# Gates, merges and the merged sum with tokens on partitions: activations stand still, weights pass 512 columns wide

## The chip, the cores and the metric

The kernel runs on one core of one Trainium2 chip. The metric is the device time of one execution in microseconds. A core has TensorE (PE, the matrix engine, which takes its instructions in order), VectorE (DVE), ScalarE (ACT), GpSimd (POOL) and SyncE (SP, which issues the DMA transfers here). They run side by side and wait for each other through semaphores.

## The reference

Two layers, each with a mixer of four branches and a mixture of experts, on 256 tokens (T) of 1024 channels (D). What matters here is the end of the mixer: each branch output is projected to 1024 channels, multiplied by a sigmoid gate computed from the layer's input h, and the four are added and projected once more.

```python
def hybrid_mixer(h, positions, w_in, ..., branch_proj, w_gate, w_out):
    ...
    merged = [jax.nn.sigmoid(h @ w_gate[i]) * (o.astype(h.dtype) @ branch_proj[i])
              for i, o in enumerate((o_gdn, o_ret, o_nsa, o_fox))]
    y = merged[0] + merged[1] + merged[2] + merged[3]
    return y @ w_out
```

## The kernel before, in words

Channels lie on partitions throughout the mixer: h is held as 8 blocks (k) of 128 channels by 256 tokens. Matmuls of single-precision accuracy are made of three passes in a faster format: every operand is split into a rounded part and a rest (`hh`/`hl` for h, `whi`/`wlo` for a weight, `yh`/`yl` for the merged sum, `gdnhi`/`gdnlo` and the like for a branch's output, `bhi`/`blo` for a branch's projection), and hi x hi, lo x hi and hi x lo are added in PSUM. ACT makes the rounded part of a weight and DVE the rest (`split_half`), 512 columns at a time; a part holds 1024 columns, and one part is ahead of its use.

A matmul names the operand that stands still (its weight load is an instruction of its own) and the one that passes; a profile row `ps_d<-hh,whi` has the passing one first. In the gates (`gates`, through `dense_T` and `dense_k`) the weight stands still, 128 columns of it, and 256 tokens pass: for each of the 4 branches (n) and each quarter of the channels (q) 8 x 2 x 3 = 48 matmuls of 256 columns. ACT turns the result into tanh (`sg`, sigmoid up to a factor and an addend). `merge` makes the branch's projection of that quarter (12 matmuls), and DVE multiplies it by the gate (`sg`) and adds it to the sum `ymix`; for branch 3 `fin` then writes `yh` and `yl` with ACT and DVE. The output projection w_out reads them, block k after block k.

PE's order is written by hand. The branches are generators (`gdn`, `nsa`, `ret`, `fox`) driven by `drive`; between their steps `fill` takes a fixed number of steps of the filler (`s.later`): first the remaining input projections, then the gates, with steps of the conditioning vector's matmuls (`ada`) in between. A gate step is two blocks k (12 matmuls). At most `NSG` = 5 gate results wait for their merge, which needs its branch's output (`oT[n]`). What is left when the last branch (`fox`) has ended runs without anything in between (`s.ended`), then w_out and the normalisation, then the experts. On the other engines a scheduler sets the order; weight splits have high priority there. PSUM has 8 banks, of which 3 carry the tag "d" (gates, merges, `ada`, w_out) and 2 the tag "t" (transposes). SP issues the weight loads in program order through four ring buffers; loads of expert weights (`exp_w`) follow as buffers of the mixer come free.

Of the kernel before, what the change touches and what calls it, by code (L numbers as in the profile page):

```python
# [22 lines left out]
L = 2  # L23
# [15 lines left out]
MP = 9  # L39
# [116 lines left out]
def pack(inputs):  # L156
# [20 lines left out]
    wg = i["w_gate"].reshape(L, 4, KT, 128, 4, 256).transpose(0, 1, 4, 3, 2, 5)  # L177
# [48 lines left out]
class K:  # L226
# [72 lines left out]
    def split_half(s, w, pool, bufs=2):  # L299
# [7 lines left out]
        return [t.rearrange("p (k n) -> p k n", k=4) for t in (hi, lo)]  # L307
# [7 lines left out]
    def dense_T(s, act, ps, tok=False):  # L315

        for half in range(2):
            hi, lo = s.parts.pop(0)
            s.split()
            for k4 in range(4):  # L320
                k = half * 4 + k4
                s.dense_k(hi[:, k4], lo[:, k4], k, act, ps, tok)
                if k % 2 and k < 7:
                    yield

# [216 lines left out]
    def gates(s, l, act, oT, fin):  # L542
# [7 lines left out]
        def prepare():  # L550

            if len(parts) < min(NBP, len(todo)) and todo[len(parts)] in sg and ready(todo[len(parts)][0]):
                n, q = todo[len(parts)]
                if q == 0:
                    bp[n] = s.load(s.I["bp"][l, n]).rearrange("p (k n) -> p k n", k=2)
                parts.append(s.merge_split(bp[n][:, :, q * 256:q * 256 + 256]))

        def merge():
            n, q = todo.pop(0)
            s.merge(parts.pop(0), n, q, sg.pop((n, q)), oT[n])  # L560
            if n == 3:
                fin(q)

        todo = [(n, q) for n in range(4) for q in range(4)]
        for n in range(4):
            for q in range(4):
                while len(sg) >= NSG:
# [5 lines left out]
                ps = s.ps("d")  # L573
                for i, _ in enumerate(s.dense_T(act, ps)):
                    if i in MMI and len(sg) >= MM and len(parts) >= (1 if s.ended else MP):
# [3 lines left out]
                g = s.ml.tile([128, 2, T], F32, name="sg", tag="sg", bufs=NSG)  # L579
                s.nc.scalar.activation(g, ps.rearrange("p (c n) -> p c n", c=2), AF.Tanh, scale=0.5)  # L580
                sg[n, q] = g
                yield
                if parts:
                    merge()
                    yield
# [30 lines left out]
    def start(s, hT, act, x, pool):  # L616
# [5 lines left out]
        def work(n):  # L622

            for _ in range(n):
                if todo:
                    i, k0 = todo.pop(0)
                    for k in (k0, k0 + 1):
                        if i == 3:
                            s.narrow_k(hT, w[3], pn, k)
                        else:  # L630
                            hi, lo = w[i][k // 4]
# [48 lines left out]
    def mixer(s, l, hT, act, x, residual, es):  # L680
        nc, I, tc = s.nc, s.I, s.tc
        pool = lambda name, side, bufs=1: tc.tile_pool(name=f"{name}{l}", bufs=bufs, side=side, reuse_waits="tile")
        with pool("wp", "left", 2) as s.wp, ExitStack() as ml:
            s.ml = ml.enter_context(pool("ml", "left"))
            rt = es.enter_context(pool("rt", "right"))
            with pool("fx", "left") as s.fx, ExitStack() as fy:
                with pool("mx", "right") as s.mx:
# [37 lines left out]
                    def fin(q):  # L725

                        k = slice(2 * q, 2 * q + 2)
                        nc.scalar.activation(yhl[0][:, k], s.y[:, k], AF.Copy, scale=0.5)
                        nc.vector.scalar_tensor_tensor(yhl[1][:, k], s.y[:, k], 0.5, yhl[0][:, k].bitcast(F32), op0=OP.mult, op1=OP.subtract)
# [62 lines left out]
    def merge_split(s, w):  # L792
        nc = s.nc
        hi = s.wp.tile([128, 2, 256], F32R, name="bhi", tag="bhi", bufs=NBP)
        lo = s.wp.tile([128, 2, 256], F32R, name="blo", tag="blo", bufs=NBP)
        with s.tc.high_priority(HP):
            nc.scalar.activation(hi, w, AF.Copy)
            nc.vector.tensor_tensor(lo, w, hi.bitcast(F32), op=OP.subtract)
        return hi, lo

    def merge(s, w, n, q, sg, oT):
# [4 lines left out]
        for c in range(2):  # L806
            o = ps[:, c * 256:c * 256 + 256]
            cs = slice(c * 128, c * 128 + 128)
            for k in range(2):
                s.mm(o, hi[:, k, cs], oT[0][:, k], k == 0 and c == 0, False)  # L810
                s.mm(o, hi[:, k, cs], oT[1][:, k], False, False)
                s.mm(o, lo[:, k, cs], oT[0][:, k], False, k == 1)
        yq = s.y[:, 2 * q:2 * q + 2]
        p3 = ps.rearrange("p (c n) -> p c n", c=2)
        if n == 0:
            nc.vector.scalar_tensor_tensor(yq, sg, 1.0, p3, op0=OP.add, op1=OP.mult)
        else:
            nc.vector.scalar_tensor_tensor(sg, sg, 1.0, p3, op0=OP.add, op1=OP.mult)
# [934 lines left out]
```

## Time and profile before

| | |
|---|---|
| Time, median of 3 runs | 1280.85 us (1280.41 to 1282.26) |
| The profiled execution: its time, its span | 1281.46 us, 1279.6 us |
| TensorE matmul busy | 1174.5 us, 92% of the span |
| TensorE weight load busy (beside matmuls) | 831.6 us, 65% |
| VectorE, ScalarE, GpSimd busy | 623.3, 429.0, 80.6 us (49%, 34%, 6%) |
| Mean granted TensorE clock | 0.971 of full speed |
| DMA | 347.94 MB, mean 272 GB/s |

The time is that of one execution outside; the span is what the profiler saw of it. Busy time counts matmuls in flight, so PE counts as busy also where its matmuls only overlap; how often they follow each other says more than how long each lasts.

### The profile page before, as it was taken

To read this page: it belongs to the slowest core of one execution; us is meant where nothing else is said; L and a number is where in the kernel's file an instruction comes from. 1 tells how busy PE (TensorE), PEld (TensorE's weight loads), DVE (VectorE), ACT (ScalarE), POOL (GpSimd) and SP (SyncE) were. 2 spreads that over 40 slices of the span, in tenths; PEclk is the share of its full clock that TensorE was granted. 3 is DMA by queue.
4 is the path that set the end of the run, shared out by engine and by line. 5 is a ranking of instruction groups with operands and counts; after the bars stand their busy time and mean duration, and the time that the engine had idled before them with its cause. 6 is when DMAs were issued, how large, how long until landed. Compare 5 with 4: busy or idle time off the path is not lost. (4 is left out here: it accounts for less than half of the span.)

```text
span 1279.6 us, 21410 instructions
## 1 busy us (share of the span) xinstructions
PE 1174.5 (92%) x8708; PEld 831.6 (65%) x8708; DVE 623.3 (49%) x1641; ACT 429.0 (34%) x889; POOL 80.6 (6%) x92
## 2 busy tenths in 40 slices
PE   6899998989997999999879999898999799999975
PEld 3788996788993444433367889688899644444332
DVE  3694437675665222222179644757467622222214
ACT  2443432464434211111154344245354431112101
POOL 1123200000001000000001411000000100000000
PEclk9999999999998999999889999998999899999998
DMA  9886646635778999998227563552567899999920
GB/s 365 318 295 228 214 169 236 255 132 198 275 288 349 379 420 419 419 420 361 82 102 254 205 222 131 184 206 104 226 239 279 311 391 415 418 420 419 419 77 33
DMA packets 49935, 347.94 MB, mean 272 GB/s; under 512 B 5664, under 2 KB 6176, under 8 KB 8480
## 3 DMA queue, kind: packets, MB, share of 16 engines
q1 hardware_dynamic: 49680, 346.17, 69.8%
q8 instruction: 72, 1.18, 0.4%
q14 instruction: 39, 0.32, 0.1%
q10 hardware_dynamic: 144, 0.27, 0.1%
HBM read 345.37 MB, written 1.05 MB: 271 GB/s over the span
## 5 line engine op out<-in xcount | busy, mean ns | idle before, releaser
L243 PE MATMUL ps_d<-hh,whi 128*128 128x256 f32 x864 | 258.7, 299 | 6.1 <-ACT whi L305 2.8
L243 PE MATMUL ps_d<-hh,wlo 128*128 128x256 f32 x864 | 248.7, 288 | 0.7 <-DVE wlo L306 0.7
L243 PE MATMUL ps_d<-hl,whi 128*128 128x256 f32 x864 | 248.3, 287 | 1.2 <-DVE hl L668 1.1
L306 DVE TENSOR_TENSOR wlo<-w,whi 128x512 fp32r<-128x512 f32 x264 | 181.1, 709 | 120.8 <-ACT whi L305 120.2
L305 ACT ACTIVATE whi<-w 128x512 fp32r<-128x512 f32 x264 | 155.6, 624 | 230.9 <-PE ps_d L243 210.8
L243 PEld LDWEIGHTS ps_d<-hh,whi 128*128 128x128 f32 x864 | 168.3, 195 | 19.7 <-issue 10.0
L243 PEld LDWEIGHTS ps_d<-hl,whi 128*128 128x128 f32 x864 | 168.8, 195 | 1.8 <-DVE hl L668 1.6
L243 PEld LDWEIGHTS ps_d<-hh,wlo 128*128 128x128 f32 x864 | 167.3, 194 | 1.2 <-DVE wlo L306 1.2
L243 PE MATMUL ps_a<-w,hidT 128*64 128x512 f32 x512 | 118.6, 598 | 0.0
L825 DVE SCALAR_TENSOR_TENSOR x<-ps_d,mod,x 128x256 f32<-128x256 f32 x144 | 60.4, 477 | 82.3 <-PE ps_d L243 82.3
L1505 DVE TENSOR_TENSOR hid<-hid,ps_a 128x512 f32<-128x512 f32 x16 | 11.0, 688 | 169.0 <-PE ps_a L243 169.0
L243 PEld LDWEIGHTS ps_a<-w,hidT 128*64 128x64 f32 x512 | 34.5, 136 | 59.4 <-issue 56.6
L243 PE MATMUL ps_b<-w,hb 128*64 128x512 f32 x256 | 66.4, 628 | 7.1 <-PEq L1658 7.1
L243 PE MATMUL ps_b<-w,XG 128*64 128x512 f32 x256 | 66.4, 621 | 0.0
L243 PE MATMUL ps_a<-w,XG 128*64 128x512 f32 x256 | 60.6, 594 | 0.0
L243 PE MATMUL ps_a<-w,hb 128*64 128x512 f32 x256 | 59.7, 592 | 0.0
L1536 ACT ACTIVATE oh<-ps_a,cw 128x512 fp32r<-128x512 f32 x30 | 20.6, 688 | 116.1 <-PE ps_a L243 86.1
L243 PEld LDWEIGHTS <-ha 128*128 128x128 bf16 x576 | 40.6, 100 | 24.2 <-issue 22.5
L1537 DVE SCALAR_TENSOR_TENSOR ol<-ps_a,cw,oh 128x512 fp32r<-128x512 f32 x30 | 22.4, 748 | 68.3 <-ACT oh L1536 68.3
L243 PE MATMUL ps_d<-P,ha 128*128 128x128 bf16 x512 | 49.9, 224 | 5.8 <-DVE P L1457 4.3
L996 POOL TENSOR_TENSOR C<-Lm,consm 128x512 f32<-128x512 f32 x28 | 39.3, 1422 | 93.3 <-PE ps_a L243 84.3
L243 PEld LDWEIGHTS ps_b<-w,hb 128*64 128x64 f32 x256 | 18.8, 143 | 38.2 <-issue 35.7
(433 smaller groups left out, 1945.2 us busy)
## 6 DMA issues: line engine op xcount, KB each, us to landing
w<-exp_w SPq DMA_DIRECT2D x192, 1024.0 KB, 12.2
w<-ada SPq DMA_DIRECT2D x48, 1024.0 KB, 5.2
w<-wg SPq DMA_DIRECT2D x32, 1024.0 KB, 4.8
w<-win SPq DMA_DIRECT2D x26, 1024.0 KB, 5.2
w<-cw SPq DMA_DIRECT2D x8, 1024.0 KB, 5.8
w<-bp SPq DMA_DIRECT2D x8, 1024.0 KB, 4.8
w<-wo SPq DMA_DIRECT2D x8, 1024.0 KB, 4.9
consm<-constm SPq DMA_DIRECT2D x2, 720.0 KB, 6.5
```

Of the source, the lines that this page charges most:

```text
L243: return s.nc.tensor.matmul(o, l, r, start=start, stop=stop, skip_group_check=True)
L305: nc.scalar.activation(hi[:, m], w[:, m], AF.Copy)
L306: nc.vector.tensor_tensor(lo[:, m], w[:, m], hi[:, m].bitcast(F32), op=OP.subtract)
L825: s.nc.vector.scalar_tensor_tensor(x[:, k], y[:, c * T:c * T + T], mod[:, 16 + k:17 + k], x[:, k], op0=OP.mult, op1=OP.add)
L996: nc.gpsimd.tensor_tensor(C[c], Lm[c], lm[:, lev][:, None].to_broadcast([128, 4, 128]), op=OP.mult)
L1505: nc.vector.tensor_tensor(t, t, hs[1], op=OP.mult)
L1536: nc.scalar.activation(oh[:, sl], po[:, sl], AF.Copy, scale=cw)
L1537: nc.vector.scalar_tensor_tensor(ol[:, sl], po[:, sl], cw, oh[:, sl].bitcast(F32), op0=OP.mult, op1=OP.subtract)
```

## The change

In gates and merges the activations now stand still (128 tokens of one block k, `hh[:, k, c]`) and the split weight passes, 512 columns wide. So a gate block is one branch (n), one half of the channels (f, 512 columns) and one half of the tokens (t); both halves t are made together by `dense_tok` into two PSUM banks, in 8 blocks k of 2 x 3 matmuls of 512 columns. A step is now one block k. w_gate is laid out for this (chunks of half of K by 512 columns). `merge` makes one half t with 6 matmuls of 512 columns; `merge_split` splits 512 columns of the projection at once, in two halves k, for both merges t. The sum `ymix` has tokens on partitions, and `fin`, which runs after each merge of branch 3, transposes its 512 channels with four PE transposes into a bank of tag "t", from which ACT and DVE write `yh` and `yl`. A new gate block of two results starts only while at most `NSG` - 2 wait. The scratch for software DMA is set to 1024 bytes.

```diff
-    wg = i["w_gate"].reshape(L, 4, KT, 128, 4, 256).transpose(0, 1, 4, 3, 2, 5)
+    wg = i["w_gate"].reshape(L, 4, 2, 4, 128, 2, 512).transpose(0, 1, 5, 2, 4, 3, 6)
...
+    def dense_tok(s, act, ps):
+        hh, hl = act
+        for k in range(KT):
+            if k % 2 == 0:
+                hi, lo = (t.rearrange("p (k n) -> p k n", k=2) for t in s.parts.pop(0))
+                s.split()
+            for t in range(2):
+                c = slice(t * 128, t * 128 + 128)
+                s.mm(ps[t], hh[:, k, c], hi[:, k % 2], k == 0, False)
+                s.mm(ps[t], hl[:, k, c], hi[:, k % 2], False, False)
+                s.mm(ps[t], hh[:, k, c], lo[:, k % 2], False, k == 7)
+            if k < 7:
+                yield
...
         def prepare():
-            if len(parts) < min(NBP, len(todo)) and todo[len(parts)] in sg and ready(todo[len(parts)][0]):
-                n, q = todo[len(parts)]
-                if q == 0:
+            if not parts and todo and todo[0] in sg and ready(todo[0][0]):
+                n, f, _ = todo[0]
+                if f == 0:
                     bp[n] = s.load(s.I["bp"][l, n]).rearrange("p (k n) -> p k n", k=2)
-                parts.append(s.merge_split(bp[n][:, :, q * 256:q * 256 + 256]))
+                parts.append(s.merge_split(bp[n][:, :, f * 512:f * 512 + 512]))
         def merge():
-            n, q = todo.pop(0)
-            s.merge(parts.pop(0), n, q, sg.pop((n, q)), oT[n])
+            n, f, t = todo.pop(0)
+            s.merge(parts[0], n, f, t, sg.pop((n, f, t)), oT[n])
+            if t:
+                parts.clear()
             if n == 3:
-                fin(q)
-        todo = [(n, q) for n in range(4) for q in range(4)]
+                fin(f, t)
+        todo = [(n, f, t) for n in range(4) for f in range(2) for t in range(2)]
         for n in range(4):
-            for q in range(4):
-                while len(sg) >= NSG:
+            for f in range(2):
+                while len(sg) > NSG - 2:
                     prepare()
                     yield
                     if parts:
                         merge()
                         yield
-                ps = s.ps("d")
-                for i, _ in enumerate(s.dense_T(act, ps)):
-                    if i in MMI and len(sg) >= MM and len(parts) >= (1 if s.ended else MP):
+                ps = [s.ps("d") for _ in range(2)]
+                for i, _ in enumerate(s.dense_tok(act, ps)):
+                    if i % 4 in MMI and len(sg) >= MM and parts and s.ended:
                         merge()
                     prepare()
                     yield
-                g = s.ml.tile([128, 2, T], F32, name="sg", tag="sg", bufs=NSG)
-                s.nc.scalar.activation(g, ps.rearrange("p (c n) -> p c n", c=2), AF.Tanh, scale=0.5)
-                sg[n, q] = g
+                for t in range(2):
+                    g = s.ml.tile([128, 512], F32, name="sg", tag="sg", bufs=NSG)
+                    s.nc.scalar.activation(g, ps[t], AF.Tanh, scale=0.5)
+                    sg[n, f, t] = g
                 yield
-                if parts:
-                    merge()
-                    yield
+                for _ in range(2):
+                    if parts:
+                        merge()
+                        yield
...
-                    def fin(q):
-                        k = slice(2 * q, 2 * q + 2)
-                        nc.scalar.activation(yhl[0][:, k], s.y[:, k], AF.Copy, scale=0.5)
-                        nc.vector.scalar_tensor_tensor(yhl[1][:, k], s.y[:, k], 0.5, yhl[0][:, k].bitcast(F32), op0=OP.mult, op1=OP.subtract)
+                    def fin(f, t):
+                        pt = s.ps("t")
+                        for i in range(4):
+                            s.tr(pt[:, i * 128:i * 128 + 128], s.y[:, t, f * 512 + i * 128:f * 512 + i * 128 + 128])
+                        p4 = pt.rearrange("p (k n) -> p k n", k=4)
+                        hi, lo = (y[:, 4 * f:4 * f + 4, t * 128:t * 128 + 128] for y in yhl)
+                        nc.scalar.activation(hi, p4, AF.Copy, scale=0.5)
+                        nc.vector.scalar_tensor_tensor(lo, p4, 0.5, hi.bitcast(F32), op0=OP.mult, op1=OP.subtract)
...
     def merge_split(s, w):
         nc = s.nc
-        hi = s.wp.tile([128, 2, 256], F32R, name="bhi", tag="bhi", bufs=NBP)
-        lo = s.wp.tile([128, 2, 256], F32R, name="blo", tag="blo", bufs=NBP)
+        hi = s.wp.tile([128, 2, 512], F32R, name="bhi", tag="bhi", bufs=NBP)
+        lo = s.wp.tile([128, 2, 512], F32R, name="blo", tag="blo", bufs=NBP)
         with s.tc.high_priority(HP):
-            nc.scalar.activation(hi, w, AF.Copy)
-            nc.vector.tensor_tensor(lo, w, hi.bitcast(F32), op=OP.subtract)
+            for k in range(2):
+                nc.scalar.activation(hi[:, k], w[:, k], AF.Copy)
+                nc.vector.tensor_tensor(lo[:, k], w[:, k], hi[:, k].bitcast(F32), op=OP.subtract)
         return hi, lo
-    def merge(s, w, n, q, sg, oT):
+    def merge(s, w, n, f, t, sg, oT):
         nc = s.nc
         hi, lo = w
         ps = s.ps("d")
-        for c in range(2):
-            o = ps[:, c * 256:c * 256 + 256]
-            cs = slice(c * 128, c * 128 + 128)
-            for k in range(2):
-                s.mm(o, hi[:, k, cs], oT[0][:, k], k == 0 and c == 0, False)
-                s.mm(o, hi[:, k, cs], oT[1][:, k], False, False)
-                s.mm(o, lo[:, k, cs], oT[0][:, k], False, k == 1)
-        yq = s.y[:, 2 * q:2 * q + 2]
-        p3 = ps.rearrange("p (c n) -> p c n", c=2)
+        c = slice(t * 128, t * 128 + 128)
+        for k in range(2):
+            s.mm(ps, oT[0][:, k, c], hi[:, k], k == 0, False)
+            s.mm(ps, oT[1][:, k, c], hi[:, k], False, False)
+            s.mm(ps, oT[0][:, k, c], lo[:, k], False, k == 1)
+        y = s.y[:, t, f * 512:f * 512 + 512]
         if n == 0:
-            nc.vector.scalar_tensor_tensor(yq, sg, 1.0, p3, op0=OP.add, op1=OP.mult)
+            nc.vector.scalar_tensor_tensor(y, sg, 1.0, ps, op0=OP.add, op1=OP.mult)
         else:
-            nc.vector.scalar_tensor_tensor(sg, sg, 1.0, p3, op0=OP.add, op1=OP.mult)
-            nc.vector.tensor_tensor(yq, yq, sg, op=OP.add)
+            nc.vector.scalar_tensor_tensor(sg, sg, 1.0, ps, op0=OP.add, op1=OP.mult)
+            nc.vector.tensor_tensor(y, y, sg, op=OP.add)
...
-                s.y = s.hp.tile([128, KT, T], F32, name="ymix", tag="h")
+                s.y = s.hp.tile([128, 2, D], F32, name="ymix", tag="h")
...
-    nc = bacc.Bacc("TRN2", target_bir_lowering=False, num_devices=1)
+    nc = bacc.Bacc("TRN2", target_bir_lowering=False, num_devices=1, dynamic_dma_scratch_size=1024)
```

Three places in the order. First PE at the end of layer 0's gates: `foxhi`/`foxlo` are the last branch's output, `rws` a small sum for the router, `yh`/`yl` with `whi`/`wlo` the first matmuls of w_out. Before:

```order
L243 MATMUL ps_d<-foxhi,blo 128x256
L243 MATMUL ps_d<-foxhi,bhi 128x256
L243 MATMUL ps_d<-foxlo,bhi 128x256
L243 MATMUL ps_d<-foxhi,blo 128x256
L243 MATMUL ps_b<-rws,cons 128x32
L243 MATMUL ps_d<-yh,whi 128x256 [waits Activation_49]
L243 MATMUL ps_d<-yl,whi 128x256 [waits DVE_49]
L243 MATMUL ps_d<-yh,wlo 128x256
```

Now:

```order
L243 MATMUL ps_d<-bhi,foxlo 128x512
L243 MATMUL ps_d<-blo,foxhi 128x512
L247 MATMUL ps_t<-cons,ymix 128x128 [waits DVE_49,PE_49]
L247 MATMUL ps_t<-cons,ymix 128x128 x3
L243 MATMUL ps_d<-bhi,foxhi 128x512 [waits Activation_49]
L243 MATMUL ps_d<-bhi,foxlo 128x512
L243 MATMUL ps_d<-blo,foxhi 128x512
L243 MATMUL ps_d<-bhi,foxhi 128x512
L243 MATMUL ps_d<-bhi,foxlo 128x512
L243 MATMUL ps_d<-blo,foxhi 128x512
L247 MATMUL ps_t<-cons,ymix 128x128 [waits DVE_49,PE_49]
L247 MATMUL ps_t<-cons,ymix 128x128 x3
```

Before, w_out's matmuls come directly behind the last merge; now four transposes of `ymix` stand behind each merge of this branch, and the first of them carries a wait for DVE.

Second DVE at the same place: line 818 before and line 839 now is the product of gate and projection, line 819 and 840 the sum, line 729 and 752 the part `yl`. Before:

```order
L818 SCALAR_TENSOR_TENSOR sg<-sg,ps_d 128x512 [waits PE_49]
L798 TENSOR_TENSOR blo<-w,bhi 128x512 [waits Activation_49]
L819 TENSOR_TENSOR ymix<-ymix,sg 128x512 [waits DVE_49]
L306 TENSOR_TENSOR wlo<-w,whi 128x512 [waits PE_49,Activation_49]
L729 SCALAR_TENSOR_TENSOR yl<-ymix,yh 128x512 [waits Activation_49] x3
L818 SCALAR_TENSOR_TENSOR sg<-sg,ps_d 128x512 [waits PE_49,Activation_49]
L306 TENSOR_TENSOR wlo<-w,whi 128x512 [waits Activation_49]
L819 TENSOR_TENSOR ymix<-ymix,sg 128x512 [waits DVE_49]
```

Now:

```order
L306 TENSOR_TENSOR wlo<-w,whi 128x512 [waits Activation_49]
L306 TENSOR_TENSOR wlo<-w,whi 128x512 [waits PE_49,Activation_49]
L752 SCALAR_TENSOR_TENSOR yl<-ps_t,yh 128x4x128 [waits Activation_49] x2
L839 SCALAR_TENSOR_TENSOR sg<-sg,ps_d 128x512 [waits PE_49]
L306 TENSOR_TENSOR wlo<-w,whi 128x512 [waits Activation_49]
L840 TENSOR_TENSOR ymix<-ymix,sg 128x512 [waits DVE_49]
L752 SCALAR_TENSOR_TENSOR yl<-ps_t,yh 128x4x128 [waits Activation_49]
L839 SCALAR_TENSOR_TENSOR sg<-sg,ps_d 128x512 [waits PE_49]
L840 TENSOR_TENSOR ymix<-ymix,sg 128x512 [waits DVE_49]
```

Before, three `yl` are written from `ymix` ahead of the last product; now two `yl` are written from transposes in PSUM ahead of the product of the merge before the last, behind which that merge's transposes wait.

Third PE in the middle of layer 0, in the compression of the sparse attention (`w,bk`) and the rotation of the retention's keys and queries (`ps_b<-c`). Before:

```order
L243 MATMUL ps_t<-w,bk_2169 32x256 x2
L243 MATMUL ps_t<-w,bk_2177 32x256 x2
L243 MATMUL ps_b<-c_106 128x256
L243 MATMUL ps_b<-c_106 128x128
L243 MATMUL ps_b<-c_106 128x256
L243 MATMUL ps_b<-c_106 128x128
L243 MATMUL ps_d<-hh,whi 128x256
L243 MATMUL ps_d<-hl,whi 128x256
L243 MATMUL ps_d<-hh,wlo 128x256
```

Now:

```order
L243 MATMUL ps_b<-c_106 128x256
L243 MATMUL ps_b<-c_106 128x128
L243 MATMUL ps_b<-c_106 128x256
L243 MATMUL ps_b<-c_106 128x128
L243 MATMUL ps_t<-w,bk_2104 32x256 x2
L243 MATMUL ps_t<-w,bk_2112 32x256 x2
L243 MATMUL ps_t<-w,bk_2104 32x256 x2
L243 MATMUL ps_t<-w,bk_2112 32x256 x2
L243 MATMUL ps_b<-c_106 128x256
```

Before, 24 gate matmuls (the last three rows are the first of them) stand between the `ps_b<-c` and the next `w,bk`; now the next `w,bk` follows at once, since four gate results wait already, and the gates that stood here come later in the program.

## Rows read from the trace of the kernel before

**Rows 1.** The page, its first part: busy us (share of the span) xinstructions.

```profile
PE 1174.5 (92%) x8708; PEld 831.6 (65%) x8708; DVE 623.3 (49%) x1641; ACT 429.0 (34%) x889; POOL 80.6 (6%) x92
```

**Rows 2.** Windows of layer 0's gate stretch: length, busy us of each engine (instructions), granted clock, DMA.

```profile
150.00:240.00 90.00, 84.73 (x736) 72.48 (x735) 48.55 (x105) 31.50 (x60) 4.06 (x7) 0.98 0.62 228
240.00:290.00 50.00, 45.85 (x356) 41.81 (x356) 38.31 (x144) 29.27 (x88) 0.00 (x0) 0.97 0.39 144
...
338.00:356.00 18.00, 17.98 (x151) 17.78 (x150) 13.03 (x22) 8.47 (x16) 0.00 (x0) 1.00 0.71 255
```

**Rows 3.** PE's waits from 150 to 356 us: total us, times, longest.

```profile
PE ps_a L243 <- DVE stn L1293: 4.0, 4, 2.8
PE ps_b L243 <- DVE c L1124: 2.9, 2, 2.0
```

**Rows 4.** Experts of layer 0: a window, and SP's timeline (start, us, operation, count).

```profile
480.00:512.00 32.00, 31.93 (x199) 14.16 (x200) 9.13 (x25) 5.53 (x12) 0.00 (x0) 1.00 1.01 420
...
379.90 210.65 SPq L262 DMA_DIRECT2D w<-exp_w  x83
```

**Rows 5.** Window of 10 us of gates and merges alone; the first count is PE's matmuls.

```profile
340.00:350.00 10.00, 9.98 (x84) 9.78 (x83) 7.41 (x12) 4.06 (x7) 0.00 (x0) 1.00 0.64 256
```

**Rows 6.** Lines by form, plain f32 matmuls: standing*, passing, count | busy us, mean ns.

```profile
L243 PE MATMUL ps_a<-w,hidT 128*64 128x512 f32 x512 | 118.6, 598 | 0.0
...
L247 PE MATMUL ps_t<-cons,XTV 128*128 128x128 f32 x96 | 12.8, 276 | 0.0
...
L243 PE MATMUL ps_t<-w,bk 128*32 128x256 f32 x128 | 8.5, 384 | 0.0
```

**Rows 7.** Timeline of PE: 32 plain f32 matmuls of 152 columns in a row.

```profile
664.44 4.29 PE L243 MATMUL ps_d<-w,h 128*128 128x152 f32 x32
```

**Rows 8.** Timeline of PE, first and last of 15 matmuls in a row.

```profile
270.94 0.41 PE L243 MATMUL ps_d<-gdnlo,bhi 128*128 128x256 f32 x1
...
273.92 0.41 PE L243 MATMUL ps_d<-hh,whi 128*128 128x256 f32 x1
```

**Rows 9.** Timeline: eight transposes; and a PE matmul behind the DVE operation it waits for.

```profile
321.29 1.03 PE L247 MATMUL ps_t<-cons,E 128*128 128x128 f32 x8
...
219.99 0.42 DVE L1124 TENSOR_TENSOR c<-ps_b,c 128x256 f32<-128x256 f32 x1
220.47 0.92 PE L243 MATMUL ps_b<-c 64*128 64x256 f32 x4 [2.04 <-DVE c L1124]
```

**Rows 10.** Timeline: a merge's last matmul and its product; a product, a split, a sum.

```profile
338.32 0.28 PE L243 MATMUL ps_d<-nsahi,blo 128*128 128x256 f32 x1
338.64 0.69 DVE L818 SCALAR_TENSOR_TENSOR sg<-sg,ps_d 128x512 f32<-128x512 f32 x1 [0.20 <-PE ps_d L243]
...
343.27 0.68 DVE L818 SCALAR_TENSOR_TENSOR sg<-sg,ps_d 128x512 f32<-128x512 f32 x1
343.87 0.68 DVE L798 TENSOR_TENSOR blo<-w,bhi 128x512 fp32r<-128x512 f32 x1
344.47 0.68 DVE L819 TENSOR_TENSOR ymix<-ymix,sg 128x512 f32<-128x512 f32 x1
```

**Rows 11.** Tiles `sg` and `ymix`: durations in ns (least/median/most), first and last start.

```profile
L580 ACT ACTIVATE sg<-ps_d x32: 577/580/598, 178.4 to 977.3; 128x512 f32<-128x512 f32 x32
L819 DVE TENSOR_TENSOR ymix<-ymix,sg x24: 679/684/685, 283.3 to 979.5; 128x512 f32<-128x512 f32 x24
L728 ACT ACTIVATE yh<-ymix x8: 615/616/617, 355.2 to 980.7; 128x512 fp32r<-128x512 f32 x8
```

**Rows 12.** Timeline of PE: the first two matmuls of w_out in layer 0.

```profile
356.11 0.36 PE L243 MATMUL ps_d<-yh,whi 128*128 128x256 f32 x1
356.63 0.39 PE L243 MATMUL ps_d<-yl,whi 128*128 128x256 f32 x1 [0.15 <-DVE yl L729]
```

**Rows 13.** Timeline of a long wait of PE; and a window (granted clock third from the end).

```profile
269.62 0.79 PE L243 MATMUL ps_a<-ks,nq 64*128 64x144 f32 x4 [2.82 <-DVE stn L1293]
...
272.00:273.00 1.00, 1.00 (x6) 1.00 (x6) 0.12 (x1) 1.00 (x8) 0.00 (x0) 0.50 0.43 57
```

More of the change, by code (lines that the diff above doesn't have):

```diff
@@ L38 @@
 MMI = (1, 2)
-MP = 9
 RDY = 10
@@ L306, in split_half @@
                 nc.vector.tensor_tensor(lo[:, m], w[:, m], hi[:, m].bitcast(F32), op=OP.subtract)
-        return [t.rearrange("p (k n) -> p k n", k=4) for t in (hi, lo)]
+        return hi, lo
     def hilo(s, src, hi, lo):
@@ L317, in dense_T @@
         for half in range(2):
-            hi, lo = s.parts.pop(0)
+            hi, lo = (t.rearrange("p (k n) -> p k n", k=4) for t in s.parts.pop(0))
             s.split()
@@ L630, in work @@
                         else:
-                            hi, lo = w[i][k // 4]
+                            hi, lo = (v.rearrange("p (k n) -> p k n", k=4) for v in w[i][k // 4])
                             s.dense_k(hi[:, k % 4], lo[:, k % 4], k, act, ps[i])
```

## The prediction

> **What bounds the kernel now.** I read the page's busy shares first, then the windows, then the timeline. TensorE (PE) is busy 92% of the span [rows 1], and in the stretch where the gates run it is busy almost without a gap: 84.7 of 90 us, 45.9 of 50, 18.0 of 18 [rows 2]. So a matmul that is cheaper there is worth something, and a wait of PE there costs its full length, unless a chain of VectorE (DVE) and ScalarE (ACT) work is what PE waits for anyway. That is so between 240 and 290 us, where DVE is busy 38.3 of 50 us and PE waits 4.0 us in all for the softmax sums `stn` [rows 2, 3]. Behind the mixer the expert weights run at 420 GB/s, and most of them are only issued from the mixer's end on [rows 4]; their stream starts when the mixer's buffers come free, so what the mixer gains or loses moves everything behind it. I count the mixer's difference once per layer and carry it through whole. GpSimd issues no DMA here, so the smaller DMA scratch costs nothing.
>
> **What it removes.** Per layer 768 gate and 192 merge matmuls of 256 columns become 384 and 96 of 512: 480 pairs turn into 480 single ones. What is a pair worth? 84 gate matmuls take 10 us: 119 ns each [rows 5]. Plain f32 costs (598-384)/256 = 0.836 ns a column and (384-276)/128 = 0.84 [rows 6], two steps of 0.417 at 2.4 GHz; 152 such columns are 126.7 ns of streaming, and the 32 of them, each with its own 128-column weight load, follow each other every (4.29-0.29)/31 = 129 ns [rows 7]. So some 2.4 ns lie over the streaming when it is long; 256 columns stream in 107 and yet take 119. That is a floor, not a surcharge: where the clock was at 1.2 GHz the same matmuls came every (273.92-270.94)/14 = 213 ns, just 256 columns at that clock [rows 8]. So 512 columns should take 213.3+2.4 = 216, against 2x119 = 238: 22.4 ns saved for each pair. The bounds are 0 (512 at twice 119) and 25 (no surcharge); I take 22.4, since rows 7 is the nearest row. For both layers 960 pairs x 22.4 ns = 21.5 us, if all is kept.
>
> A rule speaks against this. The Trainium skill (TensorE: Matmul & The Clock Gate, "Back-to-back issue gap" and "LDWEIGHTS") gives N/2.4 + 2.5 ns for a matmul and 128/1.2 = 107 ns for the load, so that 256 columns would take an estimated 109 and a pair would save only 2.5 ns, 2.4 us in all. No row here has 109; rows 5 has 119, and the measurement decides.
>
> **What of it is kept.** The gates are filler, taken in a fixed number of steps between the steps of the branches. The old and new steps are alike (12 of 256, 6 of 512 columns), but a block of gates now needs two free slots of five, so in the order the filler runs dry earlier. At the last product with the forgetting attention's values 156 gate and 96 merge matmuls were left in both layers; now, counted in old ones, 216 and 108 in layer 0 and 192 and 108 in layer 1. The stretch after it, where PE has nothing else, therefore grows: 252 x 0.119 = 30.0 us becomes 162 x 0.2157 = 34.9 and 150 x 0.2157 = 32.4, a loss of 4.9+2.4 = 7.3. The filler shrinks from 708 x 0.119 = 84.3 us in each layer to 318 x 0.2157 = 68.6 and 330 x 0.2157 = 71.2: 15.7+13.1 = 28.8 less. (28.8-7.3 is the 21.5 again.) Of the 28.8 PE gets back only what no chain takes: nearly all where it is never late, about half between 240 and 290. I keep 78%, 22.4; the bounds are 50% (14.4) and all. Gain: 22.4-7.3 = 15.1, between 7.1 and 21.5.
>
> **What it adds on PE.** (a) 16 transposes a layer at (1.03-0.27)/7 = 0.108 us [rows 9]: 1.75 us.
>
> (b) The wait before them. PE works in order, and each group of four transposes stands right behind the merge whose sum it reads. A merge's last matmul of 256 columns at 338.32 let DVE start at 338.64 [rows 10]: 0.32, and 107 ns more for 512 columns, 0.43. Then the product 0.69 and the sum 0.68 on DVE [rows 10, 11], and 0.06 from DVE's end to PE's start, as 219.99+0.42 to 220.47 [rows 9]. That is 1.87 us after the last matmul's start, where PE would have gone on after 0.22: **1.65 us** at the least, four times a layer. Before, this chain ended in yh and yl, and the first output block of w_out covered it: PE lost only 0.4 us there (356.11 to 356.63) [rows 12].
>
> In two of the four DVE's order makes it longer. Behind the second merge of the first half a blo split stands between product and sum, as it does now at 343.87 (0.60) [rows 10]: 2.25. Behind the first merge of the second half the two yl of the first half come ahead of the product, and they wait for ACT. From the start R of the last gate matmul: tanh ends at R+0.4, a whi at R+0.95, the two yh at R+2.15 (0.58 to 0.62 each [rows 11]), the second yl at R+2.9, the product at R+3.5, a wlo at R+4.1, the sum at R+4.75; PE could have been there at 7 x 0.216 = R+1.5, so it waits 3.3. Sum of the four: 1.65+2.25+3.3+1.65 = 8.85 us a layer.
>
> (c) The clock. A wait of 2.82 us for DVE left the granted clock at 0.5 for the 15 matmuls after it [rows 8, 13]: 14 x (0.213-0.119) = 1.3 us. One such place a layer (the 3.3 followed by 1.65): 1.0, between 0 and 2.5. At that level the pair saves nothing, 2 x 213 against 427.
>
> (d) PSUM: gates now hold two of the three "d" banks, so merges follow each other through the third, each waiting for the product before it (0.43+0.69 against 6 x 0.216 = 1.3 us of matmuls in between): 0.5 a layer, between 0 and 1.5. (e) The old tail wait goes: -0.5.
>
> The work of DVE and ACT stays what it was: as many tanh, products, sums and splits of 512 columns, four yh and yl a layer. They cost nothing of their own; PE's matmuls hide them as before, and if that cover went they would cost the 0.6 to 0.7 of each.
>
> Sum per layer: 1.75+8.85+1.0+0.5-0.5 = 11.6; both layers 23.2. Against the gain of 15.1 that is +8.1. The profiled execution took 1281.46 (0.6 over the median), so 1289.6, and by the median **1289 us**.
>
> **The rivals.** (1) *Faster: the filler's saving is kept whole and the tail's waits stay at their floor.* The place is ACT and DVE at the end of the gates: if yh and yl of the first half are done before the last merge's product is due, all four waits are 1.65. Then a layer loses 1.75+6.6-0.5 = 7.85, 15.7 in all, against 21.5: 1275 by the median. For it: joins between 150 and 240 us have little waiting. Against: the order of DVE. It decides from 9.5 us lost a layer downward. (2) *No change*: whole gain (21.5) and waits as worked out (23.2), 1282; anything between that and rival 1. (3) *The branches take the filler's saving*: at half kept the gain is 7.1, the time 1297. For it: DVE's 77% from 240 to 290 and its waits [rows 2, 3]; against: PE is not late elsewhere. (4) *The pair saves nothing*: what lies over 107 ns is paid per column, 512 take 238, and the gates' change does not do what it says. Gain 0, waits stay: 1304. Rows 8 speak against it.
>
> **How the numbers follow.** A measurement of this kernel tells 0.2%, about 2.6 us, from no change. Forecast 0.55, rival (1) 0.18, (2) 0.14, (3) 0.10, (4) 0.03. Slower is forecast, (3) and (4): 0.68; same 0.14; faster 0.18. The forecast's own range, from its bounds, is 1284 to 1295. For 8 in 10 I go down to 1276, which takes in (2) and about half of (1), and up to 1300, which takes in (3).
>
> **What would show it.** Right: gate matmuls of 512 columns every 0.216 us; in each layer four waits of PE for the sum at the transposes, the third over 3 us, 8 to 9 us in all; a granted clock of 0.5 near the end of the gates; fewer gate matmuls before the last branch step and a longer stretch after it. Wrong: a pitch near 0.238, or waits under 6 us a layer; a mixer that ends earlier than before although PE waits would mean that more than 78% was kept. A product that PE reaches late because PSUM is not free would show as waits for ACT's tanh at the gates' first matmuls.

## The result, and the profile after

The changed kernel takes 1311.62 us (median of 4 runs, 1310.33 to 1314.61), the kernel before 1280.75: a ratio of 1.0242, 95% interval 1.0222 to 1.0262. The direction was right; 30.9 us slower lies outside the forecast range, whose upper end was 1300.

The page after, busy shares (against [rows 1]) and the granted clock in 40 slices:

```profile
PE 1183.2 (90%) x7780; PEld 780.3 (60%) x7780; DVE 624.0 (48%) x1641; ACT 427.5 (33%) x889; POOL 80.6 (6%) x92
...
PEclk9999999899888999999889999988998999999988
```

928 matmuls fewer (960 saved, 32 transposes added), and yet PE is busy longer. The timeline of PE after, the places that answer to [rows 5, 8 to 10, 12]:

```profile
315.66 1.52 PE L243 MATMUL ps_a<-PT,fv 128*64 128x256 f32 x16
...
331.52 0.40 PE L243 MATMUL ps_d<-whi,hh 128*128 128x512 f32 x1
...
341.13 0.40 PE L243 MATMUL ps_d<-wlo,hh 128*128 128x512 f32 x1
341.36 0.39 PE L243 MATMUL ps_d<-bhi,foxhi 128*128 128x512 f32 x1
...
342.50 0.39 PE L243 MATMUL ps_d<-blo,foxhi 128*128 128x512 f32 x1
344.76 0.63 PE L247 MATMUL ps_t<-cons,ymix 128*128 128x128 f32 x4 [1.87 <-DVE ymix L840]
...
351.80 0.63 PE L247 MATMUL ps_t<-cons,ymix 128*128 128x128 f32 x4 [2.08 <-DVE ymix L840]
352.19 0.48 PE L243 MATMUL ps_d<-whi,hh 128*128 128x512 f32 x1
...
353.16 0.63 PE L243 MATMUL ps_d<-whi,hh 128*128 128x512 f32 x1
...
355.30 0.63 PE L243 MATMUL ps_d<-wlo,hh 128*128 128x512 f32 x1
...
365.32 0.63 PE L247 MATMUL ps_t<-cons,ymix 128*128 128x128 f32 x4 [2.94 <-DVE ymix L840]
...
369.64 1.09 PE L247 MATMUL ps_t<-cons,ymix 128*128 128x128 f32 x4 [1.60 <-DVE ymix L840]
...
370.81 0.56 PE L243 MATMUL ps_d<-yh,whi 128*128 128x256 f32 x1
...
953.81 1.52 PE L243 MATMUL ps_a<-PT,fv 128*64 128x256 f32 x16
1006.09 0.56 PE L243 MATMUL ps_d<-yh,whi 128*128 128x256 f32 x1
```

Three things are to be seen. From 331.52 to 341.13 there are 42 gate matmuls, 41 distances: 0.234 us each, not 0.216 (the merge's six: (342.50-341.36)/5 = 0.228; other merges of this trace come every 0.228 to 0.232). Each group of transposes waits for the sum, 1.87, 2.08, 2.94 and 1.60 us. And behind the second wait the same gate matmuls come every (355.30-353.16)/5 = 0.43 us. The windows show the clock there and over the last 30 us of the end (columns as in [rows 2], the granted clock third from the end):

```profile
353.00:355.00 2.00, 2.00 (x6) 1.54 (x6) 0.08 (x1) 0.74 (x2) 0.00 (x0) 0.50 0.83 221
...
341.00:371.00 30.00, 21.51 (x82) 16.34 (x81) 13.42 (x21) 8.54 (x16) 0.00 (x0) 0.81 0.45 145
```

PE's waits after (total us, times, longest): first from 750 us to the last product with the forgetting attention's values in layer 1 (955.4), then from there to 1010:

```profile
PE ps_d L243 <- ACT bhi L821: 2.4, 2, 1.7
...
PE ps_d L243 <- DVE blo L822: 2.0, 2, 1.6
...
PE ps_t L247 <- DVE ymix L840: 8.5, 4, 3.0
PE ps_d L243 <- ACT bhi L821: 0.5, 1, 0.5
PE ps_d L243 <- DVE blo L822: 0.4, 2, 0.2
```

The waits for the split of the projection (`bhi`, `blo`) are new: 4.4 us ahead of that product and 0.9 behind it in layer 1, and 2.4 ahead of it in layer 0 (2.1 and 0.3), 7.7 in all; before there were none.

To compare kernels I cut the span at marks of PE. The *fill* is from the first `ps_a<-XTV,C` (layer 1: `ps_d<-w,h`) to the end of the last `ps_a<-PT,fv`, the *end of the gates* from there to the first `ps_d<-yh,whi`, then the *output projection* up to its last matmul. So the end of layer 0's gates after is 370.81-(315.66+1.52) = 53.6 us.

| us | fill 0 | end 0 | proj. 0 | fill 1 | end 1 | proj. 1 | median |
|---|---|---|---|---|---|---|---|
| before | 216.0 | 30.9 | 28.4 | 281.3 | 30.9 | 28.4 | 1280.75 |
| after | 208.9 | 53.6 | 28.3 | 278.0 | 50.8 | 28.1 | 1311.62 |
| halves of 256 | 210.3 | 52.8 | 28.4 | 281.1 | 53.7 | 28.2 | 1319.98 |
| no transposes | 209.2 | 38.2 | 28.2 | 280.5 | 36.8 | 28.2 | 1287.17 |
| later transposes | 211.0 | 41.9 | 27.3 | 280.5 | 40.5 | 27.3 | 1289.41 |
| matmuls in the waits | 208.6 | 48.8 | 27.3 | 278.3 | 47.4 | 27.3 | 1301.35 |
| six slots | 216.4 | 41.8 | 28.3 | 282.1 | 43.5 | 27.3 | 1301.86 |
| later, six slots | 214.0 | 31.7 | 27.3 | 282.1 | 33.1 | 27.3 | 1275.92 |
| the same in halves | 216.2 | 32.4 | 27.3 | 277.8 | 33.8 | 27.3 | 1278.22 |
| the same with cover | 214.0 | 28.9 | 28.1 | 278.8 | 30.3 | 28.1 | 1273.08 |

The ends grow by 22.7 and 19.9, the fills shrink by 7.1 and 3.3: 32.2 together, of 29.4 in the span; what lies outside them (start, output projections and experts) is 2.8 shorter. One profile is one execution: that of e1_pitch below, where gates and branches are the same program as after, has 209.8, 50.9, 29.5, 278.3, 50.9 and 28.1. So where PE waits for the sum, a difference of 1 to 3 us in one column is not to be read as an effect; where it hardly waits the ends repeat (30.9 and 30.9 again in e12_before_scratch).

### The profile page after: what moved, and what is told of

Read it like the earlier page. It is cut to its first block, busy times and chain, and to the rows that moved or that the text cites. A ratio compares the mean times of both kernels' runs of the same rounds, so it can differ in the third digit from the quotient of the medians.

```text
span 1309.0 us, 19529 instructions
## 1 busy us (share of the span) xinstructions
PE 1183.2 (90%) x7780; PEld 780.3 (60%) x7780; DVE 624.0 (48%) x1641; ACT 427.5 (33%) x889; POOL 80.6 (6%) x92
## 5 line engine op out<-in xcount | busy, mean ns | idle before, releaser
L243 PE MATMUL ps_d<-whi,hh 128*128 128x512 f32 (+1 forms) x320 | 128.9, 403 | 0.0
L243 PE MATMUL ps_d<-wlo,hh 128*128 128x512 f32 (+1 forms) x320 | 122.7, 384 | 0.5 <-DVE wlo L306 0.5
L243 PE MATMUL ps_d<-whi,hl 128*128 128x512 f32 (+1 forms) x320 | 122.4, 382 | 0.0
L243 PE MATMUL ps_d<-hh,whi 128*128 128x256 f32 x352 | 105.4, 299 | 5.6 <-ACT whi L305 2.9
L243 PE MATMUL ps_d<-hl,whi 128*128 128x256 f32 x352 | 100.4, 285 | 1.7 <-DVE hl L687 1.1
L243 PE MATMUL ps_d<-hh,wlo 128*128 128x256 f32 x352 | 100.6, 286 | 0.7 <-DVE wlo L306 0.7
L846 DVE SCALAR_TENSOR_TENSOR x<-ps_d,mod,x 128x256 f32<-128x256 f32 x144 | 60.4, 478 | 82.6 <-PE ps_d L243 82.6
L243 PEld LDWEIGHTS ps_d<-hh,whi 128*128 128x128 f32 x352 | 67.5, 192 | 13.7 <-issue 5.8
L243 PEld LDWEIGHTS ps_d<-hl,whi 128*128 128x128 f32 x352 | 67.9, 193 | 2.5 <-DVE hl L687 1.6
L243 PEld LDWEIGHTS ps_d<-whi,hl 128*128 128x128 f32 x320 | 62.5, 195 | 10.4
L243 PEld LDWEIGHTS ps_d<-hh,wlo 128*128 128x128 f32 x352 | 67.2, 191 | 1.2 <-DVE wlo L306 1.2
```

The source lines that it names most:

```text
L243: return s.nc.tensor.matmul(o, l, r, start=start, stop=stop, skip_group_check=True)
L846: s.nc.vector.scalar_tensor_tensor(x[:, k], y[:, c * T:c * T + T], mod[:, 16 + k:17 + k], x[:, k], op0=OP.mult, op1=OP.add)
```

## The experiments

**1. The pitch by itself (e1_pitch).** Behind the last output:

```diff
+                    for i in range(48):
+                        m(o[i % 2], a[:, i % 4], w, **K)
+                    for i in range(48):
+                        m(o[i % 2][:, 0:256], a[:, i % 4], w[:, 0:256], **K)
...
```

> The changed kernel with a block of matmuls of its own behind the last output, when every other engine is idle: 48 in a row, twice each, of the single-precision format with 512, 384, 256 and 128 passing columns and 128 standing, with 64 standing and 512 or 256 passing, and of bf16 with 512 and 256. The time itself grows by the block (some 120 to 150 us) and says nothing. In the changed kernel 512 columns were paced at 0.234 us where the forecast had 0.216. Theory R (a rate per passing column of this format, 0.457 ns): 512 at 0.234, 384 at 0.176, 256 at 0.117 also here, the same with 64 standing. Rival T (traffic of the other engines in the gate stretch slows a rate that is 0.417 ns): 512 at 0.216 in this quiet block. Rival W (the weight load takes a share): with 64 standing the 512 come at 0.220 or less. bf16 tells whether bytes count: 0.216 for 512 if they do, 0.234 if not.

The time is 1427.03 us, with the block. The timeline of PE in it (lines 1774 to 1788 are the loops; the rows of `pw` are fp32r, the format of the gates, which the trace names f32):

```profile
1356.33 5.47 PE L1788 MATMUL ps_d<-pw,pa 128*128 128x128 f32 x48
1361.64 11.11 PE L1774 MATMUL ps_d<-pw,pa 128*128 128x512 f32 x48
1372.59 5.92 PE L1776 MATMUL ps_d<-pw,pa 128*128 128x256 f32 x48
1378.34 8.49 PE L1778 MATMUL ps_d<-pw,pa 128*128 128x384 f32 x48
1386.90 10.31 PE L1780 MATMUL ps_d<-pwb,pab 128*128 128x512 bf16 x47
1397.04 5.40 PE L1782 MATMUL ps_d<-pwb,pab 128*128 128x256 bf16 x48
1402.20 11.30 PE L1784 MATMUL ps_d<-pw,pa 128*64 128x512 f32 x48
1413.34 5.63 PE L1786 MATMUL ps_d<-pw,pa 128*64 128x256 f32 x48
1418.80 5.47 PE L1788 MATMUL ps_d<-pw,pa 128*128 128x128 f32 x48
...
1345.00:1420.00 75.00, 74.93 (x470) 59.71 (x469) 0.00 (x0) 0.00 (x0) 0.00 (x0) 1.00 0.00 1
```

The last line is a window: the other engines and the DMA are idle, the granted clock is 1.00. From start to start: fp32r 512 columns (1372.59-1361.64)/48 = 0.228, 256 columns 0.120, 384 columns 0.174 (one bf16 record is missing, so 0.216 is taken off first); bf16 512 columns 10.14/47 = 0.216. At 2.4 GHz the columns alone are 213, 107, 160 and 213 ns. So fp32r pays 13 to 15 ns **for each matmul** at these three lengths, and bf16 2.5. Theory R falls in its form (a rate would give 0.176 and 0.234). W falls for 512 columns (64 standing: 11.14/48 = 0.232, no faster); with 256 columns, 64 standing come every (1418.80-1413.34)/48 = 0.114, so there about 6 of the 13 ns go with the standing columns.

Rival T is not settled by this block alone: 512 columns take 0.228 in it and 0.234 in the gates, where 256 take 0.119 to 0.120 as here. Two places in the traces speak against traffic as the reason, first one of the kernel after, then one of experiment 5, where seven matmuls repeat one pair of operands:

```profile
982.14:983.07 0.93, 0.93 (x5) 0.75 (x4) 0.00 (x0) 0.00 (x0) 0.00 (x0) 1.00 0.00 0
982.14 0.39 PE L243 MATMUL ps_d<-whi,hl 128*128 128x512 f32 x1
...
983.08 0.39 PE L243 MATMUL ps_d<-wlo,hh 128*128 128x512 f32 x1
...
341.40:343.00 1.60, 1.60 (x8) 1.11 (x6) 1.56 (x3) 0.00 (x0) 0.00 (x0) 1.00 1.02 430
341.38 1.75 PE L244 MATMUL ps_t<-bhi,foxhi 128*128 128x512 f32 x7
```

With every other engine and the DMA idle the gate matmuls still come every (983.08-982.14)/4 = 0.235; beside a busy DVE and 430 GB/s the repeated ones come every (1.75-0.39)/6 = 0.227. So the 6 ns go with the gate matmuls themselves. What in them it is (operands that change from one to the next, or the adding up in one bank), no run separates.

**2. Halves (e2_split256).**

```diff
-                s.mm(ps[t], hh[:, k, c], hi[:, k % 2], k == 0, False)
+                for m in (slice(0, 256), slice(256, 512)):
+                    s.mm(ps[t][:, m], hh[:, k, c], hi[:, k % 2, m], k == 0 and m.start == 0, False)
...
```

> The changed kernel with each gate and merge matmul of 512 columns made of two of 256, everything else as in the change. If a pair saves only 2 x 0.119 - 0.234 = 4 ns, as the pitch in the changed kernel says, 960 pairs give 3.8 us at most: 1311 to 1316 us. If the wide matmul did save what was forecast (22.4 ns a pair, 21.5 us) and something else ate it, this goes to 1326 to 1334.

Measured 1319.98 (1316.11 to 1320.89), ratio 1.0288 (1.0266 to 1.0310): 8.4 us more than the change, in neither of the two ranges: over what 4 ns a pair give and far under 22.4. In the table layer 0 (fill and end) differs by 0.6 and layer 1 by 6.0, part of it in longer waits (`bhi` and `blo` 5.9 in its fill, against 4.4) and in matmuls at half clock behind them. So this run puts the pair's worth far under 22.4 ns (8.4/960 = 9 ns if all of it were the pair's) and does not fix it.

**3. No transposes (e3_no_transpose).**

```diff
-                        pt = s.ps("t")
-                        for i in range(4):
-                            s.tr(pt[:, i * 128:i * 128 + 128], s.y[:, t, f * 512 + i * 128:f * 512 + i * 128 + 128])
-                        p4 = pt.rearrange("p (k n) -> p k n", k=4)
+                        p4 = s.y[:, t, f * 512:f * 512 + 512].rearrange("p (k n) -> p k n", k=4)
```

> The changed kernel without the transposes of the merged sum: the parts yh and yl are written from the sum as it lies, so the output differs; PE no longer waits for the sum behind each merge. Theory E (the end of the gates costs: waits of 8.5 us a layer, transposes 1.75, and matmuls at half the granted clock behind the waits, 4.7 and 3.2 us): 17.0 + 3.5 + 7.9 = 28.4 us less, 1283 us, between 1280 and 1288. Rival F (the gates pushed behind the last branch make the stretch longer, and the waits only move to the output projection): 1296 or more.

Measured 1287.17, ratio 1.0045 (1.0030 to 1.0059): 24.4 us less, in the range of theory E. The end of layer 0's gates is 38.2 us: that is the 162 wide matmuls left there at 0.234 (37.9) and nothing else. Its `yh` and `yl` hold the sum untransposed, so its output is not the reference's; the time is what counts here. So the transposes with all that hangs on them cost 53.6-38.2 = 15.4 us there and 50.8-36.8 = 14.0 in layer 1; the rest of the ends is the filler that was pushed behind the branch.

**4. Later transposes (e4_late).** They stand two steps behind their merge, and the last two groups behind the last merge:

```diff
             if n == 3:
-                fin(f, t)
+                late.append((steps[0], f, t))
...
+                    steps[0] += 1
+                    flush(2)
```

> The changed kernel with each group of four transposes put later: those of the first half two steps (12 or more matmuls of 512) behind their merge, those of the second half both behind the last merge. Same work. Theory E: the first two waits go (1.9 + 2.1), the third falls from 2.9 to about 1.5 and the fourth stays at 1.2 to 1.6, so 8.5 becomes about 2.9 a layer, and of the matmuls at half clock some 3 us a layer go: 2 x (5.6 + 3) = 17 us less, 1294 us, between 1290 and 1299. Rival F: the chain of ScalarE and VectorE at the end of the gates decides, since yh can be written only when the last gate matmul is through, and the time stays within 3 us of 1311.

Measured 1289.41 (1284.97 to 1292.34), ratio 1.0058 (1.0036 to 1.0081): 22.2 us back, more than expected. One wait is left in each layer's end:

```profile
PE ps_t L247 <- DVE ymix L848: 1.6, 1, 1.6
```

So 6.9 us of waiting went in each layer (I had expected 5.6), and with it the half clock, which does not follow the wait that is left: the ends are 11.7 and 10.3 shorter. Rival F is out: the chain of ACT and DVE does not hold the end.

**5. Matmuls in the waits (e5_warm).** The wait stays, but PE is busy in it:

```diff
+                        for _ in range(NW[f, t]):
+                            s.mm(pt, oT[3][0][:, 0, 0:128], s.bhi[:, 0], True, True)
                         for i in range(4):
                             s.tr(pt[:, i * 128:i * 128 + 128], s.y[:, t, f * 512 + i * 128:f * 512 + i * 128 + 128])
```

> The changed kernel with 7, 8, 11 and 6 extra matmuls of 512 columns, which read what is there and whose result is overwritten, ahead of the four groups of transposes: PE is busy where it waited for the sum, and the sum comes no sooner. If the matmuls at half the granted clock behind the waits cost what their pitch says (4.7 and 3.2 us against 0.6 in each layer before), 6.7 us go: 1305 us, between 1302 and 1308. Rival: the clock does not follow the waits, or the work behind them is late anyway: within 2 us of 1311.6.

Measured 1301.35 (1299.82 to 1304.98), ratio 1.0178 (1.0162 to 1.0194): 10.3 us less, just under the range. The granted clock over the end of the gates, against 0.81 after:

```profile
341.00:366.00 25.00, 24.10 (x118) 19.27 (x117) 14.08 (x23) 8.55 (x16) 0.00 (x0) 1.00 0.47 169
```

The ends shrink by 4.8 and 3.4, the output projections, whose first matmuls had been at half clock, by 1.0 and 0.8: 10.0. The extra matmuls do no work for the result. The transposes start sooner behind their merges by 0.65 us a layer in sum, 1.3 in all, so some 8.7 of the 10.0 are the price of the clock; I had expected 6.7.

**6 and 7. Six slots (e6_six_slots), and with later transposes (e7_late_six).**

```diff
-NSG = 5
+NSG = 6
```

> The changed kernel with 6 slots for gate results instead of 5, so that a block of two may start while four wait, and the order of the fill comes near that of before. In the changed kernel PE waits in the fill for the split of the projection (bhi, blo) 2.4 us in layer 0 and 5.3 us in layer 1, since a blocked gate step leaves no matmuls between a split and its merge. If the two-slot rule is the cause, these go: some 7 us less, 1304, between 1301 and 1307. Rival: the waits come from the split being twice as long, and stay: 1309 or more.

> Both edits: the later transposes (1289.4 us measured) and six slots. If the two losses are apart from each other, 7 us less than with the later transposes alone: 1282, between 1279 and 1285, level with the kernel before. Rival (the slots are not the cause of what is left in the fill): 1287 or more.

Six slots alone: 1301.86 (1301.14 to 1304.41), ratio 1.0180 (1.0165 to 1.0194), 9.8 us less. More gates are back in the fill (fills longer by 7.5 and 4.1, ends shorter by 11.8 and 7.3). The waits for `bhi` and `blo` are gone from both fills; what is left in layer 1 (750 to 956 us, all of it) was there before too, but for the last line:

```profile
PE ps_a L243 <- DVE stn L1314: 5.0, 3, 2.1
PE ps_b L243 <- DVE c L1145: 2.8, 2, 1.9
PE ps_a L243 <- ACT sh L1227: 2.2, 2, 1.3
PE ps_b L243 <- DVE c L1134: 1.5, 1, 1.5
PE ps_d L243 <- DVE wlo L306: 0.2, 1, 0.2
```

Both edits: 1275.92 (12 runs, 1272.98 to 1279.24), ratio 0.9965 (0.9952 to 0.9978), below the kernel before and 13.5 us below e4_late where I expected 7, and under the range. The waits for `bhi` and `blo`, which are gone here, had been 8.4 us in e4_late, so 1.4 of the surplus of 6.5 are theirs. The ends are 31.7 and 33.1, near the 30.9 of before. The fill explains part of the rest at most: 3 us between profiles of one order (282.1 here, 278.8 in e8_cover, where fill 1 is the same program) are as large as what is sought.

**8. Cover (e8_cover), the best version.**

```diff
+            for _ in range(2):
+                next(g2[0])
+            s.flush()
+            for _ in range(2):
+                next(g2[1])
```

> As before this one (later transposes, six slots), and the last two groups of transposes stand behind the first 12 matmuls of the output projection's first block, with the first 12 of its second block behind them (weights of the output projection laid out for this order). The last wait for the sum (1.6 us a layer) and the wait for yh and yl behind the last transposes get 2.8 us of matmuls as cover: 2 to 3 us less a layer, 1277 us, between 1275 and 1280. Rival: ScalarE and VectorE, which must also split the weights of these blocks, are late instead, and it stays within 1.5 us of the one without.

Measured 1273.08 (1270.84 to 1274.84), ratio 0.9946 (0.9931 to 0.9960): faster than both kernels, and under the range, since e7_late_six was so already. The last eight transposes come without a wait, between the first half of the projection's first block and the first half of its second (24 matmuls each, 2.8 us; the 12 of the expectation were a miscount):

```profile
353.19 0.37 PE L245 MATMUL ps_d<-yh,whi 128*128 128x256 f32 x1
...
356.15 1.03 PE L249 MATMUL ps_t<-cons,ymix 128*128 128x128 f32 x8
356.94 0.36 PE L245 MATMUL ps_d<-yh,whi 128*128 128x256 f32 x1
```

End and projection together fall by 2.0 us in each layer (59.0 to 57.0, 60.4 to 58.4); the medians by 2.8 for both, less than the 2 to 3 a layer expected.

**9 to 12. Controls.** The kernel of 7 in halves of 256, as in 2 (e9_late_six_split); the kernel before with six slots (e10_before_six); the best version with seven (e11_cover_seven); and the kernel before with the smaller DMA scratch (e12_before_scratch).

```diff
-NSG = 6
+NSG = 7
...
-    nc = bacc.Bacc("TRN2", target_bir_lowering=False, num_devices=1)
+    nc = bacc.Bacc("TRN2", target_bir_lowering=False, num_devices=1, dynamic_dma_scratch_size=1024)
```

> The changed kernel with later transposes and six slots (1275.9 us measured), each gate and merge matmul of 512 columns made of two of 256. Here PE hardly waits at the end of the gates, so the clock and the splits disturb less than in the first run with halves (1320.0 against 1311.6). If a pair is worth 0.238 - 0.234 = 4 ns, 960 pairs give 3.8 us and this takes 1279 to 1282. If it is worth the forecast 22.4 ns: 1297.

> The kernel before with six slots for gate results (the place comes from the smaller DMA scratch). A control: does what is gained over the kernel before by later transposes and six slots (4.5 us by the medians) come from the slots? If the slots only mend what the block of two had broken, the kernel before does not change: 1279 to 1283. If a sixth slot is worth something by itself: 1278 or less, down to 1275.

> The best version so far (later transposes, six slots, first blocks of the output projection as cover; 1273.1) with seven slots. If six slots already let the fill run as before, nothing is left to mend: within 2 us of 1273. If gate results still wait for a place: 1270 or less.

> The kernel before with the smaller DMA scratch alone. The forecast put it at nothing, since GpSimd issues no DMA: within 0.2% of the kernel before, 1278 to 1283.

e9: 1278.22 (12 runs), ratio 0.9977 (0.9966 to 0.9987), 2.3 us over e7 and just under the range, so 960 pairs are worth some 2.4 ns each (between 1 and 4 by the scatter of the runs), less than the 4 and a tenth of the forecast. Its timeline has 24 gate matmuls of 256 columns with the activation standing, 23 distances:

```profile
336.77 0.28 PE L243 MATMUL ps_d<-whi,hh 128*128 128x256 f32 x1
...
339.47 0.28 PE L243 MATMUL ps_d<-wlo,hh 128*128 128x256 f32 x1
```

0.117 us each, against 0.119 in [rows 5] with the weight standing: what the change saves on a gate pair comes with the exchange of the operands, and the width adds nearly nothing (2 x 0.117 = 0.234). Whether it is the operand that stands or the order that goes with it, no run separates.

e10: 1279.62, ratio 0.9990 (0.9979 to 1.0001), no change that can be told; e12: 1280.43, ratio 0.9999 (0.9987 to 1.0010). Neither the slots nor the scratch are worth anything that can be told in the kernel before. e11: 1274.16, ratio 0.9935 (0.9919 to 0.9952): six slots are enough.

## Why the prediction was wrong in size

**The step that failed: what a pair saves.** "That is a floor, not a surcharge" was the error. [rows 5] had 119 ns for 256 columns, 12 over the streaming; I took the 2.4 ns of the plain f32 rows [rows 7] as this format's surcharge because they were nearest, and rows 8, where 256 columns at the lower clock take just their 213 ns, as proof that there is none. It only shows none at that clock. e1 has 13 to 15 ns on every fp32r matmul, at full clock, so by its pitches a pair saves 2 x 0.120-0.228 = 12 ns, not 22.4. In the gates 512 columns take 0.234, and this second loss, 6 ns a matmul, is measured but not explained. A gate pair therefore saves 2 x 0.119-0.234 = 4 ns and a merge pair 2 x 0.119-0.228 = 10: 768 x 4 + 192 x 10 = 5.0 us at most, not 21.5, and by e9 half of that is not the width's. Rival (4), with 3 in 100, came nearest in the number (1304), not in its mechanism: it had 512 at 238 because the surplus is paid per column, and e1 shows it paid per matmul. Its 1304 is 7.6 us short; the clock and the new wait below cost more than that, and what a pair does save takes some of it back.

The Trainium skill's rule that I weighed (TensorE: Matmul & The Clock Gate, "Back-to-back issue gap") had a pair at 2.5 ns, near the 4 measured and far from my 22.4. Its figures hold in e1 for bf16 (0.216 for 512); for fp32r they don't (0.228 and 0.120), so that the rule came near in the difference is luck.

**What of it is kept.** The counts were right: the end without transposes is the 162 wide matmuls that I had counted, at 0.234 instead of 0.2157. At that pitch the fills save at most 84.3-318 x 0.234 = 9.9 and 84.3-330 x 0.234 = 7.1 us. They gave 7.1 and 3.3. Not on my list was the wait for `bhi` and `blo`, 2.4 us in the fill of layer 0, 4.4 in that of layer 1 and 0.9 behind it: with four results waiting and a block that needs two places, the splits and their merges stand with no gate matmuls between them. The order had shown the blocked gates (the third place), and I had priced only that they come later. Six slots removed it.

**The waits before the transposes.** Right: 8.85 us forecast, 8.5 measured in each layer, in parts 1.65, 2.25, 3.3, 1.65 against 1.87, 2.08, 2.94, 1.60. DVE's order made the second and the third longer as forecast, a `blo` split ahead of the sum and two `yl` ahead of the product:

```profile
350.37 0.69 DVE L822 TENSOR_TENSOR blo<-w,bhi 128x512 fp32r<-128x512 f32 x1
350.97 0.68 DVE L840 TENSOR_TENSOR ymix<-ymix,sg 128x512 f32<-128x512 f32 x1
...
362.09 1.28 DVE L752 SCALAR_TENSOR_TENSOR yl<-ps_t,yh 128x512 fp32r<-128x512 f32 x2
363.29 0.68 DVE L839 SCALAR_TENSOR_TENSOR sg<-sg,ps_d 128x512 f32<-128x512 f32 x1
```

The transposes themselves: 2.0 (starts to the next matmul: 0.38, 0.39, 0.38, 0.88) against 1.75. The PSUM wait of 0.5 a layer was not there: in the ends PE is listed as waiting for the sum and, in layer 1, 0.9 us for the splits, not for a bank.

**The clock.** Right in kind, mis-sized: 1.0 a layer, for one place, 2.5 as its bound. In layer 0 the first two waits were each followed by eight matmuls at 0.43, the third by three and the last by the output projection's first ones at half clock, and e5 gives some 9 to 10 us for both layers. I had applied the row of one stall [rows 8, 13] to one stall of four, and with matmuls of 0.119, not 0.234. Not every such wait is followed by it: the first of layer 1 (1.85 us) was not, and in e1's profile, same gates, neither were the first two of layer 0 (its end is 50.9 there).

**The sum.** Forecast: fills -22.4, ends +7.3+23.2 = 30.5. Measured: -10.4 and +42.6. In the fills the pitch makes 17.0 of the 28.8, and the new waits there, 2.4+4.4 = 6.8, are about what is missing to the 10.4; so the 22% that I wrote off to the chains of the branches were hardly lost, as far as single profiles can tell. Of the 12.1 more in the ends, 312 wide matmuls at 0.234 instead of 0.2157 are 5.7, and the clock most of the rest.

**Open.** Why e7 and e9 beat the kernel before: e9 has the ends and projections 0.4 and 1.8 us longer than the kernel before, yet its median is 2.5 lower; 0.002 less on 1536 matmuls is 3.1, most of which must lie in the fills, and these differ by 3 us between profiles of one order, too much to show it. And the 6 ns that a gate matmul of 512 columns takes over the quiet block, of which only the traffic beside it can be ruled out.

## What to carry to other kernels

A pitch above the streaming time is to be tested at a second length of the same format before it is called a floor: 256 columns alone could not tell a floor from a surcharge, 384 and 512 did. Operations that PE itself must do on the result of another engine (here the transposes) belong some steps behind it in PE's order; the wait is paid twice, once as a wait and again in the clock behind it (17 and some 9 us here). When a unit of work takes two slots where it took one, look what stands between a producer and its consumer when the slots are full.

## What the runs showed of the hardware

In the quiet block of e1 each fp32r matmul with 128 standing columns costs 13 to 15 ns over its columns at the granted clock of 1.00, at 256, 384 and 512 columns alike, and bf16 2.5 with 512; with 128 columns and 128 standing fp32r comes every (1361.64-1356.33)/48 = 0.111 us, where the columns are 53 ns. The gates pay 0.234 for 512 columns, with and without traffic beside them. Seven of the eight waits of 1.6 to 3.0 us at the transposes of the kernel after were followed by matmuls at half clock (behind the second 0.50 was granted, and 353.16 to 355.30 are six of its eight matmuls at 0.43), one of 1.85 us was not, nor was the one of 1.6 us that e4 leaves in each layer; with matmuls in the same stretches the granted clock stayed at 1.00.
